# Attention stage of a decoder layer on one Trainium2 core: the last group's projection weights split once, the convolution's weights parked in free tiles

## The chip, the cores and the metric

The kernel runs on one core of a Trainium2 chip. The metric is the device time of one execution in microseconds (us); the median of three runs stands for a version. The engines are named as in the profile: PE does matmuls, PEld is its weight load, DVE, ACT and POOL work on tiles in on-chip memory, SP only issues DMAs. Each engine has its own queue and takes its instructions in the order that the program gives them; semaphores tell one engine that another is done.

## The reference, cut to what matters

One decoder layer works on 1024 positions of width 1024, all in float32. The part around the change is the mixing sub-layer:

```python
h = modulate(rms_norm(x, g_mix[l]), sh2, sc2)
b_g, c_g, u, q, k, v, z_conv, z_attn = jnp.split(h @ w_in[l], IN_OFFSETS, axis=-1)
y_conv = (b_g * short_conv(c_g * u, conv_w[l])) @ w_conv_proj[l]
q, k = apply_rope(q, cos, sin), apply_rope(k, cos, sin)
y_attn = sliding_window_attention(q, k, v, sinks[l]) @ w_attn_proj[l]
merged = jax.nn.sigmoid(z_conv) * y_conv + jax.nn.sigmoid(z_attn) * y_attn
x = x + gt2[:, None, :] * (merged @ w_out[l])
```

Attention has 16 heads of 64 in 4 groups of 4; a block of 128 positions sees itself and the block before it.

## The kernel before, in words

**Precision.** Every float32 matrix product is made of three matmuls on a high and a low part of each operand (`mm3`, L138, L140, L142). The parts are made by `split` (L106 and L107): ACT casts the high part, DVE subtracts it from the source for the low part. A weight block of 512 KB is loaded by `load_st` (L114) into one of four staging tiles `wr`, and `Weights` splits it into two tiles: four instructions, two on ACT and two on DVE. Loads through `parts_tile` put the parts into the 8 tiles `w`; with `tiles=` they go to tiles `t` of the pool "T", which has 28 and holds almost everything of this stage.

**The attention loop.** 32 units, (group g, block n), run through a software pipeline with a turn for each value of `s`, 0 to 36. In a turn PE does, in this order:

- stage c of unit s-3: the scores (L1031); DVE and ACT then make maximum and exponentials (L1042, L1048), POOL scales them (L1060)
- stage b of unit s-2: transposes q and k (L1010), which ACT and DVE split for the next turn's stage c
- stage a of unit s: q, k and v, 24 matmuls (L975 to L977); the last one is in turn 31
- some pieces of the output projection from the list `fill` (`proj_piece`): two a turn, one from turn 29 on, three from turn 33 on; a piece is 6 matmuls, and DVE adds it to `yat` (L1132)
- stage e of unit s-5: probabilities times v (L1097, L1098)
- stage d of unit s-4: transposes the probabilities (L1074), which ACT and DVE split for the next turn's stage e

The input of stage a, `h`, lies in 16 tiles of T, 8 for each half of the positions. The first half is last read in turn 27, the second in turn 31. When a group has finished a half, its 8 pieces enter `fill`; the pieces of group 3's first half are (3,0,0) to (3,0,7), those of the second half (3,1,0) to (3,1,7). The projection weights of a group are two blocks, `wap[g, 0]` and `wap[g, 1]`, and every half loads and splits both anew into two tiles of T each: `next_wap` runs when the piece before a block's first one has been issued, so 16 such loads in all.

**After the loop** comes `load_wc(0)`: four blocks of the convolution's projection weights through `wr`, split into the `w` tiles, which stage a's weights of group 3 hold until turn 31. Then `load_y(1)`, `conv_proj(0, 0)` and `conv_proj(1, 0)` (24 matmuls each), the eight pieces (3,1,*), and the other `conv_proj`. `load_y(0)`, 8 loads of 512 KB into T for the first half of the convolution's result, is called in turn 29 already. Each `conv_proj` also loads two stored gates (L1149) into the small tiles `r` and combines the branches on DVE (L1159 to L1161).

**What sets the order.** On PE the order is that of the code. On ACT, DVE, POOL and SP a scheduler sets it: it orders by its own estimate of when inputs and free tiles are there, so an instruction may stand ahead of its place in the code, and an engine waits whenever the estimate was too early. Each queue is served strictly in order: an ACT instruction that waits for a DMA holds every ACT instruction behind it.

Of the kernel before, what the change touches and what calls it, by code (L numbers as in the profile page):

```python
# [8 lines left out]
F32 = mybir.dt.float32  # L9
# [16 lines left out]
NKV = 4  # L26
# [9 lines left out]
def tile_macaron_layer(  # L36
# [19 lines left out]
    nc = tc.nc  # L56
# [12 lines left out]
    def nm(s):  # L69
        uid[0] += 1  # L70
        return f"{s}_{uid[0]}"

    def bank():
        return ps.tile([P, 512], F32, tag="ps", name=nm("ps"), bufs=8)
# [4 lines left out]
    def tile_t(dt=F32R, shape=(P, 2, HALF)):  # L79
        return act.tile(list(shape), dt, tag="T", name=nm("t"), bufs=28)  # L80

    def tile_c(dt, shape=(P, 1024)):
        return tile_t(dt, shape)
# [11 lines left out]
    def f32(t):  # L95
        return t.bitcast(F32)
# [4 lines left out]
    def pair_of(t):  # L101

        return t[:, 0, :], t[:, 1, :]
# [8 lines left out]
    def load_st(src):  # L112
        st = wgt.tile([P, 1024], F32, tag="wr", name=nm("wr"), bufs=4)
        nc.sync.dma_start(st[:, : src.shape[1]], src)  # L114
        return st
# [15 lines left out]
    def load_w(src, lo_engine=nc.vector, tiles=None):  # L131
        return Weights(load_st(src), src.shape[1], lo_engine, tiles)

    def mm3(outs, w, xs, start, stop):

        wh, wl = w
        for o, (xh, xl) in zip(outs, xs):
            mm(o, wh, xh, start=start, stop=False)  # L138
        for o, (xh, xl) in zip(outs, xs):
            mm(o, wh, xl, start=False, stop=False)  # L140
        for o, (xh, xl) in zip(outs, xs):
            mm(o, wl, xh, start=False, stop=stop)  # L142
# [437 lines left out]
    def load_last(hid):  # L580
        out = []
        for jj in range(2):
            out.append([])
            for h in range(2):
                t = tile_t()
                nc.sync.dma_start(f32(t), hid.last[jj][h])
                out[jj].append(pair_of(t))
        return out
# [43 lines left out]
    with tc.tile_pool(name="f1", bufs=2) as tmp:  # L632
# [150 lines left out]
        last = load_last(hid)  # L783
# [163 lines left out]
        for k in range(4):  # L947
            t = tile_t()
# [5 lines left out]
    with tc.tile_pool(name="att", bufs=2) as tmp:  # L954
# [5 lines left out]
        def load_group(g):  # L960
            lo_engine = nc.gpsimd if g == 0 else nc.vector
            wq[g] = [
                Weights(load_st(wqkv[g, kp]), 768, lo_engine,
                        )
                for kp in range(4)
            ]
# [36 lines left out]
        def stage_b(g, n):  # L1003

            u = st[g, n]
            if n == 0:
                kts[g] = tile_c(F32R), tile_c(F32R)
            o = bank()
            for i in range(3):
                nc.tensor.transpose(  # L1010
                    o[:, i * P : (i + 1) * P], u["r"][:, i * P : (i + 1) * P], ident
                )
            qt = sum_tile(HALF, F32R)
            qh, ql = qt[:, 0:256], qt[:, 256:512]
            split(qh, ql, o[:, 0:256])
            kh, kl = (t[:, n * P : (n + 1) * P] for t in kts[g])
            split(kh, kl, o[:, 256:384])
            u["q"] = (qh, ql)
# [46 lines left out]
        def stage_d(g, n):  # L1065

            u = st[g, n]
            nkb = 1 if n == 0 else 2
            ph, pl = tile_c(F32R), tile_c(F32R)
            for kb in range(nkb):  # L1070
                o = bank()
                for j in range(4):
                    at_col = (j % 2) * 2 + j // 2
                    nc.tensor.transpose(  # L1074
                        o[:, at_col * P : (at_col + 1) * P],
                        u["p"][:, j * 256 + kb * P : j * 256 + (kb + 1) * P], ident,
                    )
                split(ph[:, kb * 512 : (kb + 1) * 512], pl[:, kb * 512 : (kb + 1) * 512], o)
            u["pt"] = (ph, pl)
# [32 lines left out]
        wapt = {}  # L1112

        def next_wap(g, h, db):
            wapt["next"] = load_w(wap[g, db // 4], tiles=[tile_t(), tile_t()])

        def proj_piece(g, h, db):

            if db % 4 == 0:
                wapt[0] = wapt.pop("next")  # L1120
            o = bank()
            ah, al = at[g, h]
            for pr in range(2):
                c0 = pr * 512 + (db % 4) * P
                mm3([o], wapt[0](c0), [(ah[:, pr, :], al[:, pr, :])],
                    pr == 0, pr == 1)
            if db % 4 == 3 and fill:
                next_wap(*fill[0])
            if g == 0:
                nc.scalar.copy(yat[db][h], o)  # L1130
            else:
                nc.vector.tensor_tensor(yat[db][h], yat[db][h], o, op=ALU.add)  # L1132

        wc, yparts, stored = {}, {}, {}
# [3 lines left out]
        def load_y(h):  # L1138
            for i in range(KT):
                t = tile_t()  # L1140
                nc.sync.dma_start(f32(t), ycv[i][h])
                yparts[i, h] = pair_of(t)

        def load_wc(dq):
            wc[dq] = [load_w(wcp[g, dq]) for g in range(4)]
# [23 lines left out]
        n_units = len(units)  # L1169
        for s in range(n_units + 5):  # L1170
            def at_(k):
                return units[s - k] if 0 <= s - k < n_units else None
            if at_(3):
                stage_c(*at_(3))
            if at_(2):
                stage_b(*at_(2))
            if at_(0):
                g, n = at_(0)
                if n == 0:
                    load_group(g)  # L1180
                stage_a(g, n)
            if s == n_units - 3:
                load_y(0)

            for _ in range(2 if s < n_units - 3 else 1 if s <= n_units else 3):
                if fill:
                    proj_piece(*fill.pop(0))
            if at_(5):
                stage_e(*at_(5))
                g, n = at_(5)  # L1190
                if n % 4 == 3:
                    if not fill:
                        next_wap(g, n // 4, 0)
                    fill += [(g, n // 4, db) for db in range(8)]
            if at_(4):
                stage_d(*at_(4))
        load_wc(0)
        load_y(1)
        conv_proj(0, 0)
        conv_proj(1, 0)  # L1200
        while fill:
            proj_piece(*fill.pop(0))
# [65 lines left out]
    last = load_last(hid)  # L1268
# [146 lines left out]
```

## Time and profile before

| what | value |
|---|---|
| median of three runs | 2280.16 us (2279.49 to 2284.03) |
| the profiled execution's own time | 2279.57 us |
| its span, first to last instruction | 2277.8 us |
| busy: PE, DVE, ACT, POOL | 97%, 74%, 47%, 17% of the span |
| mean granted PE clock | 0.989 of full speed |
| turns 29 to 36 of the loop, from the trace | 1352.58 to 1422.85 us |
| the eight pieces (3,1,*) | 1433.75 to 1451.74 us |

Times in the trace are us from the start of the span. A row of the time line gives start, duration, engine, source line, operation, the tiles written and read, and in brackets the idle time before it with the work that ended the wait. Durations of matmuls that follow each other overlap; the distance between their starts is what each costs (0.23 us for 128x512 at full clock). A row of a table by stretches gives the stretch, its length, the busy time and number of instructions of PE, PEld, DVE, ACT and POOL, the granted PE clock, the share of the DMA engines and GB/s.

### The profile page before, as it was taken

How to read it: one execution, taken by the hardware profiler on the slowest of the kernel's cores; microseconds unless marked ns; L12 is line 12 of the kernel's file. 1: busy time of each engine (PE TensorE's matmuls, PEld its weight loads, DVE VectorE, ACT ScalarE, POOL GpSimd, SP SyncE). 2: the span in 40 equal slices, each digit the busy share in tenths (PEclk: the TensorE clock that was granted, in tenths of full speed). 3: DMA queues.
4: the chain of work that ended last, by engine and by line, in shares of the span. 5: the costliest groups of instructions: out<-in, count | busy, mean ns of one | idle time of the engine just before them, and what ended most of it. 6: DMA issues, size and time to landing. Idle time of an engine off the chain costs nothing.

```text
span 2277.8 us, 30045 instructions
## 1 busy us (share of the span) xinstructions
PE 2202.4 (97%) x10392; PEld 1844.5 (81%) x10392; DVE 1682.2 (74%) x2982; ACT 1062.8 (47%) x2095; POOL 382.5 (17%) x429
## 2 busy tenths in 40 slices
PE   5899999999998999999999998999999999999997
PEld 3688888888887888888999996788888888888886
DVE  8997778767867776777477878455786776676876
ACT  4554444444446534343476555124644444454443
POOL 3000000005452000000344343002100000002644
PEclk9999999999999999999999999999999999999998
DMA  8265456599832534544221233554233553389932
GB/s 322 76 222 177 147 185 213 179 405 302 278 106 103 189 117 124 157 157 131 92 64 57 63 107 103 175 178 150 70 121 120 185 185 120 121 323 346 345 113 74
DMA packets 146744, 381.63 MB, mean 168 GB/s; under 512 B 20384, under 2 KB 22560, under 8 KB 146592
## 3 DMA queue, kind: packets, MB, share of 16 engines
q1 hardware_dynamic: 141984, 371.33, 46.5%
q0 software_dynamic: 4608, 8.39, 2.1%
q8 instruction: 81, 1.33, 0.2%
q14 instruction: 71, 0.58, 0.1%
HBM read 270.61 MB, written 109.05 MB: 167 GB/s over the span
## 4 chain that ended last, share of the span: by engine, by line
PE 88%; DVE 8%; DMA 2%; issue 1%; ACT 1%; POOL 1%; SPq 0%; POOLq 0%; DVEq 0%; ACTq 0%
PE ps L195 61%; PE ps L142 6%; PE ps L138 6%; PE ps L140 6%; PE ps L977 2%; PE ps L976 2%; PE ps L975 2%; DVE w L107 1%; PE ps L1031 1%; PE ps L1074 1%; DVE t L225 1%; DMA wr<-in_w2d_dram 1%; DVE t L107 1%; PE ps L1010 1%; POOL s L319 1%
## 5 line engine op out<-in xcount | busy, mean ns | idle before, releaser
L195 PE MATMUL ps<-t,w 128*128 128x512 f32 x6468 | 1468.9, 389 | 3.8 <-DVE r L405 3.0
L195 PEld LDWEIGHTS ps<-t,w 128*128 128x128 f32 x6468 | 1213.3, 188 | 258.9 <-DVE r L405 5.2
L106 ACT CAST w<-wr 128x512 fp32r<-128x512 f32 (+1 forms) x420 | 254.9, 612 | 484.7 <-PE ps L195 364.5
L107 DVE TENSOR_TENSOR w<-wr,w 128x512 fp32r<-128x512 f32 (+1 forms) x404 | 303.8, 759 | 141.7 <-ACT w L106 140.4
L515 POOL TENSOR_TENSOR x<-x,g 128x512 f32<-128x512 f32 x96 | 145.5, 1530 | 1058.4 <-DMA t<-hs 471.0
L106 ACT CAST w<-ws 128x512 fp32r<-128x512 f32 x231 | 143.5, 621 | 249.1 <-PE ps L195 200.3
L140 PE MATMUL ps<-t,w 128*128 128x512 f32 (+1 forms) x528 | 205.7, 390 | 5.6 <-DVE t L290 5.6
L107 DVE TENSOR_TENSOR w<-ws,w 128x512 fp32r<-128x512 f32 x231 | 160.4, 698 | 40.1 <-ACT w L106 39.7
L138 PE MATMUL ps<-t,w 128*128 128x512 f32 (+1 forms) x400 | 156.9, 392 | 7.0 <-ACT t L279 7.0
L142 PE MATMUL ps<-t,w 128*128 128x512 f32 (+1 forms) x400 | 154.9, 387 | 2.0 <-DVE w L107 2.0
L140 PEld LDWEIGHTS ps<-t,w 128*128 128x128 f32 x528 | 100.9, 191 | 27.9 <-DVE t L290 8.3
L344 DVE TENSOR_TENSOR x<-x,x 128x512 fp32r<-128x512 f32 x161 | 102.6, 684 | 3.0 <-ACT x L343 2.7
L225 DVE CUSTOM_DVE_ANT_0 wr<-wr,crow_act,v 128x1024 f32<-128x1024 f32 x56 | 71.7, 1281 | 36.1 <-DMA wr<-in_wada_dram 36.1
L343 ACT CAST x<-x 128x512 fp32r<-128x512 f32 x161 | 88.7, 621 | 20.6 <-DVE x L431 8.4
L138 PEld LDWEIGHTS ps<-t,w 128*128 128x128 f32 x400 | 76.7, 192 | 24.1 <-ACT t L279 9.6
L319 POOL TENSOR_TENSOR s<-s,q 128x512 f32<-128x512 f32 (+1 forms) x48 | 56.8, 1186 | 208.6 <-ACT q L315 196.2
L142 PEld LDWEIGHTS ps<-t,w 128*128 128x128 f32 x400 | 76.9, 192 | 17.2 <-DVE w L107 2.4
L569 DVE SCALAR_TENSOR_TENSOR x<-ps,mods,x 128x512 f32<-128x512 f32 (+1 forms) x104 | 72.9, 706 | 23.6 <-PE ps L195 13.3
L975 PE MATMUL ps<-w,t 128*128 128x384 f32 x256 | 88.2, 345 | 1.2 <-DVE vt L1000 1.2
L107 POOL TENSOR_TENSOR w<-wr,w 128x512 fp32r<-128x512 f32 (+1 forms) x16 | 21.5, 1355 | 398.6 <-ACT w L106 398.6
L977 PE MATMUL ps<-w,t 128*128 128x384 f32 x256 | 85.8, 335 | 0.0
L976 PE MATMUL ps<-w,t 128*128 128x384 f32 x256 | 85.7, 335 | 0.0
(150 smaller groups left out, 2802.3 us busy)
## 6 DMA issues: line engine op xcount, KB each, us to landing
t<-hs SPq DMA_DIRECT2D x140, 512.0 KB, 9.9
hs<-x SPq DMA_DIRECT2D x277, 256.0 KB, 4.5
wr<-in_wada_dram SPq DMA_DIRECT2D x56, 512.0 KB, 3.8
wr<-in_w1gu_dram SPq DMA_DIRECT2D x44, 512.0 KB, 4.7
wr<-in_w2gu_dram SPq DMA_DIRECT2D x44, 512.0 KB, 3.6
wr<-in_wbcu_dram SPq DMA_DIRECT2D x24, 512.0 KB, 4.1
wr<-in_w1d_dram SPq DMA_DIRECT2D x22, 512.0 KB, 7.5
wr<-in_w2d_dram SPq DMA_DIRECT2D x22, 512.0 KB, 7.5
```

Source lines behind the costliest of these rows:

```text
L106: nc.scalar.copy(hi, src)
L107: lo_engine.tensor_tensor(lo, src, f32(hi), op=ALU.subtract)
L138: mm(o, wh, xh, start=start, stop=False)
L140: mm(o, wh, xl, start=False, stop=False)
L142: mm(o, wl, xh, start=False, stop=stop)
L195: mm(o, a, b, start=first, stop=last, skip_group_check=True)
L225: nc.vector.tensor_tensor_reduce(out=st, in0=st, in1=crow_act, scale=1.0, scalar=v[:, C_BADA + i : C_BADA + i + 1], op0=ALU.mult, op1=ALU. ...
L344: nc.vector.tensor_tensor(f32r(t), t, f32(hi), op=ALU.subtract)
L515: nc.gpsimd.tensor_tensor(dst, dst, r, op=ALU.add)
L975: mm(o[:, :384], xh, wh, start=k == 0, stop=False)
L976: mm(o[:, :384], xh, wl, start=False, stop=False)
L977: mm(o[:, :384], xl, wh, start=False, stop=k == KT - 1)
```

## The change

Three things change, all in the attention loop. Turn 29 (`s == n_units - 3`) loads and splits both weight blocks of group 3 into four tiles of T, kept as `wapt["last"]`; `next_wap` loads nothing for group 3, and its 16 pieces use the kept parts. The same turn loads the four raw blocks of the convolution's weights into four tiles of T (`wc_raw`), without `wr`; they are split into the `w` tiles after the loop, as before, but from those tiles. And `load_y(0)` moves from turn 29 to turn 32 (`s == n_units`). No matmul is added, removed or moved in PE's order.

```diff
         def next_wap(g, h, db):
-            wapt["next"] = load_w(wap[g, db // 4], tiles=[tile_t(), tile_t()])
+            if g < NKV - 1:
+                wapt["next"] = load_w(wap[g, db // 4], tiles=[tile_t(), tile_t()])
 
         def proj_piece(g, h, db):
 
-            if db % 4 == 0:
+            if g == NKV - 1:
+                wapt[0] = wapt["last"][db // 4]
+            elif db % 4 == 0:
                 wapt[0] = wapt.pop("next")
...
             if s == n_units - 3:
+
+                wapt["last"] = [
+                    load_w(wap[NKV - 1, dq], tiles=[tile_t(), tile_t()]) for dq in range(2)]
+                wc_raw = [tile_c(F32) for _ in range(4)]
+                for g, t in enumerate(wc_raw):
+                    nc.sync.dma_start(t, wcp[g, 0])
+            if s == n_units:
                 load_y(0)
...
-        load_wc(0)
+        wc[0] = [Weights(t) for t in wc_raw]
         load_y(1)
```

Lines below the diff's first hunk have other numbers in the changed kernel: the addition to `yat` is L1135 there, the loads of `ycv` L1144, the loads into `wc_raw` L1191.

On SP's queue before, behind the first of the two sets of eight loads of `ycv` (whose last is the first row), stand the convolution's first four weight blocks, then the 16th and last load of projection weights, then two blocks of the convolution's second weights:

```order
L1141 DMA t_12661<-ycv_5940 128x1024
L114 DMA wr_13345<-in_wcp_dram 128x1024
L114 DMA wr_13353<-in_wcp_dram 128x1024
L114 DMA wr_13361<-in_wcp_dram 128x1024
L114 DMA wr_13369<-in_wcp_dram 128x1024
L114 DMA wr_13498<-in_wap_dram 128x1024
L114 DMA wr_13749<-in_wcp_dram 128x1024
L114 DMA wr_13757<-in_wcp_dram 128x1024
L1141 DMA t_13377<-ycv_5927 128x1024
```

Now the four blocks go straight into tiles `t`, with three blocks of the second weights around them, ahead of the first set of loads of `ycv`; the rope loads are those of turns 30 and 31:

```order
L980 DMA rope_12777<-in_rope_dram 128x96
L114 DMA wr_13733<-in_wcp_dram 128x1024
L980 DMA rope_12898<-in_rope_dram 128x96
L1191 DMA t_12663<-in_wcp_dram 128x1024
L1191 DMA t_12664<-in_wcp_dram 128x1024
L1191 DMA t_12665<-in_wcp_dram 128x1024
L1191 DMA t_12666<-in_wcp_dram 128x1024
L114 DMA wr_13741<-in_wcp_dram 128x1024
L114 DMA wr_13749<-in_wcp_dram 128x1024
L1144 DMA t_12994<-ycv_5926 128x1024
```

The four loads now stand where the eight of `ycv` stood, and those come behind them and behind two staging loads that need a free `wr`.

On ACT in turns 33 and 34 before, casts of the convolution's weights (`w<-wr`) stand ahead of the casts of stage d's transposes (`t_13119`) and of the projection weights for piece (3,0,0) (`t_13176`, `t_13177`):

```order
L106 CAST w_13355<-wr_13353 128x512
L106 CAST w_13356<-wr_13353 128x512
L1104 COPY s_13112<-ps_13103 64x256 x2
L1108 CAST t_13101<-s_13112 128x2x128
L106 CAST w_13363<-wr_13361 128x512
L106 CAST w_13364<-wr_13361 128x512
L106 CAST t_13119<-ps_13121 128x512
L106 CAST t_13119<-ps_13128 128x512
L106 CAST t_13176<-wr_13178 128x512
L106 CAST t_13177<-wr_13178 128x512
```

At the same place now:

```order
L1055 ACTIVATE es_13075<-es_13075 128x4
L1104 COPY s_13136<-ps_13127 64x256 x2
L1108 CAST t_13125<-s_13136 128x2x128
L106 CAST t_13143<-ps_13145 128x512
L106 CAST t_13143<-ps_13152 128x512
L1048 ACTIVATE t_13173,den_13175<-t_13173,negm_13174 128x256 x4
```

No cast of a weight stands in turns 33 to 36 any more.

On DVE in turn 31 before, the rows behind the low part of k (`t_12203`) run on through the softmax's denominators (L1056, L1057) and rope (L985 to L991) to v's low part (L1000), stage e's sum (L1105) and the low parts of the probabilities (`t_12928`):

```order
L107 TENSOR_TENSOR t_12203<-ps_12856,t_12202 128x128
L1056 TENSOR_TENSOR den_12838<-den_12838,es_12839 128x4
L1057 RECIPROCAL den_12838<-den_12838 128x4
L985 TENSOR_TENSOR u_12892<-ps_12865,rope_12890 128x320
L988 TENSOR_TENSOR q_12893<-ps_12865,rope_12890 128x5x32
L991 TENSOR_TENSOR q_12893<-ps_12865,rope_12890 128x5x32
L1132 TENSOR_TENSOR x_9028<-x_9028,ps_12903 128x512
L1000 TENSOR_TENSOR vt_12779<-ps_12744,vt_12779 128x64
L1105 TENSOR_TENSOR s_12920<-s_12920,ps_12911 64x256
L107 TENSOR_TENSOR t_12928<-ps_12929,t_12927 128x512
```

Now, from the same low part of k on (three more subtractions of weights stand just above these rows):

```order
L107 TENSOR_TENSOR w_13352<-t_12664,w_13352 128x512
L107 TENSOR_TENSOR t_12203<-ps_12864,t_12202 128x128
L1135 TENSOR_TENSOR x_9028<-x_9028,ps_12911 128x512
L107 TENSOR_TENSOR w_13357<-t_12665,w_13357 128x512
L1056 TENSOR_TENSOR den_12846<-den_12846,es_12847 128x4
L107 TENSOR_TENSOR w_13358<-t_12665,w_13358 128x512
L107 TENSOR_TENSOR w_13363<-t_12666,w_13363 128x512
L107 TENSOR_TENSOR w_13364<-t_12666,w_13364 128x512
L1000 TENSOR_TENSOR vt_12787<-ps_12752,vt_12787 128x64
L1057 RECIPROCAL den_12846<-den_12846 128x4
L1105 TENSOR_TENSOR s_12928<-s_12928,ps_12919 64x256
L107 TENSOR_TENSOR t_12936<-ps_12937,t_12935 128x512
```

All eight subtractions of the convolution's first weights now stand in turn 31, the last four ahead of v's low part and of the low parts of the probabilities that stage e of turn 32 reads. The four subtractions of group 3's projection weights stand in turn 29, behind its L1042.

## The prediction

> **What bounds the kernel now.** I read the page first: its first lines, and of the 40 slices the one of PE.
>
> ```profile
> span 2277.8 us, 30045 instructions
> PE   5899999999998999999999998999999999999997
> ```
>
> PE is the bound nearly everywhere; the 25th slice (1367 to 1424 us), the end of the attention loop, is one of the few with an 8. So I read that stage: the table by stretches, cut at the starts of turns 29 to 32, at the first piece of turn 33, at the first matmul of conv_proj(0, 0), and at both ends of the pieces (3,1,\*).
>
> ```profile
> 1352.58:1360.87 8.29, 8.29 (x59) 7.73 (x59) 6.32 (x22) 4.68 (x16) 3.38 (x7) 1.00 1.01 405
> 1360.87:1369.64 8.77, 8.77 (x63) 8.21 (x63) 6.87 (x23) 5.45 (x18) 2.52 (x6) 1.00 0.16 66
> 1369.64:1378.33 8.69, 8.69 (x61) 8.13 (x61) 6.56 (x23) 5.16 (x18) 5.11 (x11) 1.00 0.01 2
> 1378.33:1387.31 8.98, 6.13 (x53) 5.17 (x53) 8.26 (x25) 7.33 (x23) 0.88 (x2) 1.00 0.19 58
> 1387.31:1422.85 35.54, 27.48 (x144) 22.07 (x142) 27.65 (x61) 19.02 (x50) 10.71 (x16) 0.86 0.41 141
> 1422.85:1433.75 10.90, 10.90 (x50) 9.01 (x49) 2.85 (x6) 1.14 (x3) 0.73 (x1) 1.00 1.04 403
> 1433.75:1451.74 17.99, 14.21 (x49) 10.86 (x48) 12.88 (x21) 2.29 (x4) 0.00 (x0) 0.81 0.61 198
> 1451.74:1480.00 28.26, 28.26 (x126) 23.42 (x125) 12.07 (x18) 2.66 (x5) 0.00 (x0) 1.00 0.29 82
> ```
>
> PE is full in turns 29 to 31 and in the two conv_proj at 1422.85. It is idle for 2.85 us in turn 32, 8.06 us up to conv_proj and 3.78 us in the last row but one, and in the last two of these three rows the granted clock is below 1 as well. The waits of PE over 1352 to 1480 us name the lines, and the time line of PE the places (with the rows from which I take lengths below):
>
> ```profile
> PE ps L138 <- ACT t L106: 7.6, 2, 5.5
> PE ps L142 <- DVE t L107: 4.1, 3, 2.2
> PE ps L1031 <- ACT t L106: 2.1, 1, 2.1
> PE ps L1031 <- DVE t L107: 0.8, 1, 0.8
> ```
>
> ```profile
> 1385.06 0.38 PE L1031 MATMUL ps<-t,ws 64*128 64x256 f32 x2 [2.07 <-ACT t L106]
> ...
> 1392.48 1.04 PE L1074 MATMUL ps<-ident,t 128*128 128x128 f32 x8
> 1393.45 0.98 PE L1031 MATMUL ps<-t,ws 64*128 64x256 f32 x12
> 1394.35 0.50 PE L138 MATMUL ps<-t,t 128*128 128x512 f32 x1
> ...
> 1401.54 0.79 PE L138 MATMUL ps<-t,t 128*128 128x512 f32 x1 [5.52 <-ACT t L106]
> ...
> 1404.99 0.79 PE L142 MATMUL ps<-t,t 128*128 128x512 f32 x1 [2.23 <-DVE t L107]
> 1405.58 0.63 PE L138 MATMUL ps<-t,t 128*128 128x512 f32 x1
> 1406.01 0.63 PE L140 MATMUL ps<-t,t 128*128 128x512 f32 x1
> ...
> 1410.10 1.04 PE L1074 MATMUL ps<-ident,t 128*128 128x128 f32 x8
> ...
> 1410.89 0.47 PE L138 MATMUL ps<-t,t 128*128 128x512 f32 x1
> ...
> 1417.70 0.48 PE L138 MATMUL ps<-t,t 128*128 128x512 f32 x1
> ...
> 1421.88 0.29 PE L1097 MATMUL ps<-t,vt 128*128 128x256 f32 x1
> ...
> 1441.42 0.50 PE L138 MATMUL ps<-t,t 128*128 128x512 f32 x1 [2.07 <-ACT t L106]
> ...
> 1443.86 0.79 PE L142 MATMUL ps<-t,t 128*128 128x512 f32 x1 [1.71 <-DVE t L107]
> ```
>
> The waits at 1401.54 and 1404.99 are those of piece (3,0,0) for its weights, high part from ACT and low part from DVE; those at 1441.42 and 1443.86 are piece (3,1,4)'s for the same reason. After each pair the matmuls start 0.43 us apart (1405.58, 1406.01), not 0.23, until PE has worked for some us. Why ACT was late shows its time line, and SP's:
>
> ```profile
> 1398.86 1.14 ACT L106 CAST w<-wr 128x512 fp32r<-128x512 f32 x2 [1.26 <-DMA wr<-in_wcp_dram]
> ...
> 1400.86 1.15 ACT L106 CAST t<-wr 128x512 fp32r<-128x512 f32 x2
> ```
>
> ```profile
> 1350.11 4.10 SPq L1141 DMA_DIRECT2D t<-ycv  x8
> 1383.35 17.81 SPq L114 DMA_DIRECT2D wr<-in_wcp_dram  x4
> ```
>
> The eight loads of the convolution's result took eight tiles of T at 1350, 73 us before their use at 1422.85. Group 3's projection weights found no tile, so they lay unsplit in `wr`; the convolution's weights then waited for a `wr`, one after another from 1383 on; and ACT, whose order has their casts ahead of the projection's, stood still for each. The DMA is the head of a chain that ends at PE.
>
> **The change part by part.** The sum is made against the profiled execution (2279.57 us, span 2277.8); the median shown is 0.6 us above it.
>
> *Turns 33 to 36.* Group 3's weights are split in turn 29, and in turns 33 to 36 ACT and DVE no longer have a weight in their rows. If PE waits for nothing from 1387.31 to 1422.85, it has to do four sets of three pieces (4.18 each, 1417.70 to 1421.88), four stages e (0.97 each, from there to 1422.85), stage d once ahead of scores (0.97, 1392.48 to 1393.45) and twice ahead of pieces (0.79 each, 1410.10 to 1410.89), and one stage c (0.90, 1393.45 to 1394.35): 16.72 + 3.88 + 0.97 + 1.58 + 0.90 = 24.05, of 35.54. That is 11.5 us saved, slow clock included. What is late next is DVE: 27.65 busy in that stretch, less the splits of (3,0,0), (3,0,4) and (3,1,0) and of the four convolution blocks, which go elsewhere. The rows for a weight's low part, grouped by form over 1340 to 1425 us, give each:
>
> ```profile
> L107 DVE TENSOR_TENSOR t<-wr,t 128x512 fp32r<-128x512 f32 x10 | 7.5, 793 | 0.0
> L107 DVE TENSOR_TENSOR w<-wr,w 128x512 fp32r<-128x512 f32 x8 | 5.6, 724 | 3.8 <-ACT w L106 3.8
> ```
>
> Six at 0.79 and eight at 0.72: 27.65 - 4.7 - 5.8 = 17.1 of 24.05, a share of 71%, less than in turns 29 to 31 where PE was full (6.32 of 8.29 is 76%, 6.87 of 8.77 is 78%). So I count no wait here.
>
> *Pieces (3,1,\*).* Their weights stay from turn 29 on. The same 48 matmuls of the same size took 10.90 in the two conv_proj, here 17.99: 7.1 us saved. Between them DVE also adds in order behind waits for gate loads, but two conv_proj and six pieces fill the eight `ps` tiles, and the adds need only keep within that; in the last row of the table, with the same gate loads, PE waited for none of it. The gate loads stand behind the second set of `ycv` loads as before. I count nothing, with 0 to 2 us as bounds (the longest wait of PE in that stretch, 2.07).
>
> *Turns 29 to 32, where the splits go.* Turn 29 gets four low parts, 4 x 0.79 = 3.2 us, on a DVE that is busy for 6.32 of 8.29: 1.2 too much, which turn 30 with 1.9 free takes up. Stage c of turn 30 needs k's low part, which stands behind them; by the durations it comes just in time. 0 to 1.2 us, I take 0. Turn 31 gets eight at 0.72, 5.8 us, on 2.1 free, so DVE enters turn 32 some 3.7 late, with 8.26 to do there. Stage e of turn 32 reads the probabilities' low parts, which stand behind those eight; so PE waits in turn 32, as it does before for another reason. If DVE never idles over both turns and all its work counts, they take 6.56 + 5.8 + 8.26 = 20.6 instead of 8.69 + 8.98 = 17.67: 2.95 us lost. If no wait is left, 2.85 are gained. Not all of DVE's work stands ahead of what PE waits for last (k's low part for stage c of turn 33); going down the rows I come to 1.3 us lost, near the upper end because DVE hardly idles. That is an estimate from those rows.
>
> *What is moved on SP.* The four raw loads go out at about 1350, where the `ycv` loads did, and are read from 1372 on; those needed 8 issues in 4.10 us, these need 4. Cover 20 us. `load_y(0)` now stands behind two staging loads (each waits for a split of turn 29, by about 1360) and needs the second half of `h` (PE past stage a of turn 31, before 1378.33) and two of the tiles whose splits are in turn 31. So it issues from 1378 to 1385, and is needed at some 1413: the cover is still over 25 us, against 17.81 for four loads one after the other at 1383. Two loads of 512 KB, four casts and four subtractions are gone: nothing, ACT and DVE have room after turn 32.
>
> *Sum.* 11.5 + 7.1 - 1.3 = 17.3 us: 2279.57 - 17.3 = 2262.3 for a profiled execution, and with the 0.6 above it 2263 for the median.
>
> **The clock.** Three stretches of the table bear on what the wait of turn 32 costs:
>
> ```profile
> 1384.00:1386.00 2.00, 0.38 (x2) 0.19 (x2) 2.00 (x7) 1.47 (x5) 0.00 (x0) 1.00 0.72 213
> 1398.00:1400.00 2.00, 0.00 (x0) 0.00 (x0) 0.49 (x1) 1.14 (x3) 0.41 (x1) 0.64 0.09 35
> 1441.40:1443.80 2.40, 0.73 (x2) 0.30 (x2) 2.40 (x5) 0.49 (x1) 0.00 (x0) 0.82 0.57 148
> ```
>
> Waits of 2.07 and 0.78 with two matmuls between left the clock at 1.00; 2.07 and 1.71 with 0.73 of work between did not (0.82). I expect in turn 32 two waits of about 2 us with one piece (1.4 us) between, nearer to the first case. If the clock falls, some 13 matmuls at 0.20 more each cost 2.7 us. The Trainium skill, "TensorE: Matmul & The Clock Gate", section "Part 1: The HAM clock gate (the "warmup" mystery)", says that PE falls to half clock after at least one idle window of about 3.4 us of a free-running count. By that rule no fall would come here, since neither wait is that long; the trace disagrees in the last row above, where no unbroken 3.4 us of idle lay before the fall. By the rule the sum stays 17.3, by the rows it can be 14.6.
>
> **The rivals.**
>
> - *The clock falls in turn 32* (12%): the 2.7 us above, 2265.7. For it speaks the row at 1441.40, against it the row at 1384.00.
> - *DVE is the bound in turns 29 to 33* (14%): each wait makes the next. Then 2.95 instead of 1.3, 1.2 in turn 29, 2 at the gates and the clock's 2.7: 7.6 more, 2270. For it speak the 8.26 of 8.98 in turn 32; against it the 2.1 and 1.9 free in turns 30 and 31.
> - *No wait is left in turn 32* (5%): 2.85 gained instead of 1.3 lost, 2259.
> - *Another link is just as late* (4%): stage d's casts, behind the same DMA waits on ACT, hold stage e, or the convolution's weights are late from `t` too; the waits move instead of going, and under 4.5 us is left, 2276 to 2280. Against it: in the new rows no ACT cast of turns 33 to 36 waits for a DMA.
> - *Slower: the late `load_y(0)`* (3%). It was 73 us early, and is now in a queue behind loads that wait for splits. If SP is held until after 1427, the tiles land after 1435, PE stands before conv_proj(0, 0) for over 22 us, and that decides: from there on it is slower than before by over 4.6. At 1440 the time is 2290. Only a wait of SP for something of turn 36 could do this, and I find none in the rows.
>
> That the change does not do what it says is excluded by the program: 14 loads of projection weights are left of 16.
>
> **How the numbers follow.** The forecast with its small bounds holds 62%, and 2263 is its value. No wait left gives 2259, rounded down for the run-to-run half us to 2258.5; the second rival gives 2270. From 2258.5 to 2270 over 8 in 10 are held; left out are the last two rivals and the tail of the second. About 0.2% (4.6 us) is what a measurement of this kernel can tell from no change. Faster by more: the forecast, the first three rivals, less a little, 92%; within: 5%; slower: 3%.
>
> **What would show it.** In the changed profile PE has no wait at L138 or L142 for L106 or L107 of a weight; turn 32 shows waits at L1097/L1098 or a piece's first matmul, 3 to 5 us in turns 32 and 33; from the first piece of turn 33 to conv_proj(0, 0) 24 to 25 us; the pieces (3,1,\*) 10.9 to 11.2; the clock at 1.00 from 1387 on. It is wrong if waits of over 3 us stand in turns 33 to 36, if stage c of turn 30 waits, or if conv_proj(0, 0) waits for a DMA.

## The result, and the profile after

The changed kernel takes 2264.07 us (median of four runs, 2263.03 to 2266.09), the kernel before, beside it on the same chip, 2281.85: a ratio of 0.992, with a 95% interval of 0.9908 to 0.9932. The profiled execution took 2263.03 us, with a span 16.5 us shorter than before. From the page of the profile, its first line and the 40 slices of PE:

```profile
span 2261.3 us, 30036 instructions
PE   5899999999998999999999999999999999999997
```

The 25th slice, an 8 before, is a 9. The table by stretches, cut at the same places of the program as before (turns 29 to 32, turns 33 to 36, two conv_proj, and the pieces (3,1,\*)):

```profile
1352.91:1361.20 8.29, 8.29 (x58) 7.73 (x57) 7.86 (x24) 6.87 (x20) 1.12 (x3) 1.00 0.80 305
1361.20:1369.97 8.77, 8.77 (x62) 8.21 (x62) 7.38 (x26) 5.38 (x18) 4.63 (x9) 1.00 0.18 65
1369.97:1378.73 8.76, 8.76 (x62) 8.20 (x61) 8.53 (x25) 8.18 (x23) 4.04 (x7) 1.00 0.47 165
1378.73:1388.53 9.80, 6.61 (x54) 5.27 (x53) 9.74 (x30) 8.06 (x25) 3.62 (x6) 1.00 0.75 288
1388.53:1412.73 24.20, 24.20 (x144) 20.88 (x142) 19.55 (x51) 11.89 (x36) 8.41 (x16) 1.00 0.64 227
1412.73:1423.63 10.90, 10.90 (x50) 9.01 (x49) 2.13 (x4) 1.15 (x3) 0.74 (x1) 1.00 0.44 147
1423.63:1434.51 10.88, 10.88 (x49) 9.01 (x48) 10.68 (x18) 1.25 (x2) 0.00 (x0) 1.00 0.47 155
```

Read the second number (the stretch's length) against PE's busy time beside it: they are equal in every row but that of turn 32. Turns 33 to 36 went from 35.54 to 24.20 us, the pieces (3,1,\*) from 17.99 to 10.88, turn 32 from 8.98 to 9.80, and the clock is 1.00 throughout. From turn 29 to the end of the pieces that is 81.60 us after 99.16, 17.6 less; the span gained 16.5, so 1.1 us went elsewhere, outside these turns and pieces, in parts where PE does the same work. In the profiles of this study turn 29 begins anywhere from 1351.3 to 1355.0 us, though nothing ahead of it was changed in any of them. So I compare kernels by this stage, and by their medians. Two executions far from the rest, one of wc_raw (2782 us, granted clock 0.752) and one of the kernel before (3607 us, 0.576), are left out of the medians and ratios of the table further down.

From 1340 to 1470 us PE still waits at three places:

```profile
1381.24 0.50 PE L138 MATMUL ps<-t,t 128*128 128x512 f32 x1 [1.05 <-DVE vt L1000]
1384.45 0.39 PE L1098 MATMUL ps<-t,vt 128*128 128x256 f32 x1 [1.20 <-DVE t L107]
1387.43 0.86 PE L1031 MATMUL ps<-t,ws 64*128 64x256 f32 x10 [0.94 <-DVE t L107]
```

All three are in turn 32 and at the start of 33, and all end with DVE. The time line of DVE shows why:

```profile
1379.17 1.88 DVE L107 TENSOR_TENSOR w<-t,w 128x512 fp32r<-128x512 f32 x3
1380.98 0.21 DVE L1000 TENSOR_TENSOR vt<-ps,vt 128x64 fp32r<-128x64 f32 x1
...
1383.71 0.68 DVE L107 TENSOR_TENSOR t<-ps,t 128x512 fp32r<-128x512 f32 x1
```

The last three subtractions of the convolution's weights end at 1381.05, 2.3 us into turn 32, and v's low part (L1000), for which PE waits, stands right behind them. The matmul that waits reads only tiles `t`: what it lacks is the `ps` tile that L1000 still has to read. SP's queue:

```profile
1351.42 1.75 SPq L1191 DMA_DIRECT2D t<-in_wcp_dram  x4
1358.55 1.61 SPq L114 DMA_DIRECT2D wr<-in_wcp_dram  x2
1373.54 5.11 SPq L1144 DMA_DIRECT2D t<-ycv  x8
```

The late `load_y(0)` issues from 1373.5 to 1378.7; `conv_proj(0, 0)` starts at 1412.73 and waits for nothing.

### The profile page after: what moved, and what is told of

Read it like the earlier page. It is cut to its first block, busy times and chain, and to the rows that moved or that the text cites. A ratio compares the mean times of both kernels' runs of the same rounds, so it can differ in the third digit from the quotient of the medians.

```text
span 2261.3 us, 30036 instructions
## 1 busy us (share of the span) xinstructions
PE 2196.2 (97%) x10392; PEld 1842.2 (81%) x10392; DVE 1680.0 (74%) x2978; ACT 1061.2 (47%) x2091; POOL 382.3 (17%) x429
## 4 chain that ended last, share of the span: by engine, by line
PE 89%; DVE 7%; issue 1%; DMA 1%; ACT 1%; POOL 1%; SPq 0%; POOLq 0%; DVEq 0%; ACTq 0%
PE ps L195 63%; PE ps L138 6%; PE ps L142 6%; PE ps L140 6%; PE ps L977 1%; PE ps L975 1%; PE ps L976 1%; DVE w L107 1%; PE ps L1031 1%; DVE t L225 1%; PE ps L1074 1%; DMA wr<-in_w2d_dram 1%; DVE t L107 1%; POOL s L319 1%; DVE x L569 1%
## 5 line engine op out<-in xcount | busy, mean ns | idle before, releaser
L142 PEld LDWEIGHTS ps<-t,w 128*128 128x128 f32 x400 | 76.7, 192 | 17.3 <-DVE w L107 2.4
```

## The experiments

All twelve kernels do the whole computation. The table gives, in us, the stretches of each profile as above; the ratios are against runs of the kernel before on the same chip (median 2281.4 to 2282.9 us beside the other kernels). Labels are shortened to their words.

| kernel | 29-32 | 33-36 | conv | (3,1,\*) | sum | median | ratio, 95% |
|---|---|---|---|---|---|---|---|
| before | 34.7 | 35.5 | 10.9 | 18.0 | 99.2 | 2281.85 | 1 |
| changed | 35.6 | 24.2 | 10.9 | 10.9 | 81.6 | 2264.07 | 0.9908-0.9932 |
| changed, again | 35.6 | 24.2 | 10.9 | 10.9 | 81.5 | 2264.57 | 0.9915-0.9942 |
| y_only | 32.9 | 32.5 | 10.9 | 18.5 | 94.8 | 2279.31 | 0.9974-0.9993 |
| y_after_loop | 35.7 | 35.1 | 13.0 | 20.5 | 104.2 | 2286.36 | 1.0014-1.0033 |
| wc_raw | 35.6 | 28.3 | 10.9 | 17.8 | 92.6 | 2275.62 | 0.9958-0.9984 |
| wap_once | 35.6 | 24.2 | 10.9 | 10.9 | 81.5 | 2262.91 | 0.9891-0.9927 |
| first_half | 35.6 | 24.1 | 10.9 | 17.6 | 88.3 | 2269.64 | 0.9939-0.9968 |
| y_last | 36.7 | 24.2 | 10.9 | 10.9 | 82.6 | 2267.04 | 0.9918-0.9955 |
| wc_lo_pool | 37.0 | 25.2 | 10.9 | 10.9 | 84.0 | 2267.58 | 0.9914-0.9946 |
| raw_late | 34.5 | 28.0 | 10.9 | 10.9 | 84.3 | 2267.82 | 0.9926-0.9959 |
| half_raw | 33.3 | 26.0 | 10.9 | 10.9 | 81.1 | 2263.40 | 0.9909-0.9933 |
| raw_t34 | 32.9 | 29.4 | 10.9 | 10.9 | 84.1 | 2266.73 | 0.9920-0.9945 |
| raw_t35 | 32.9 | 24.9 | 10.9 | 10.9 | 79.5 | 2262.99 | 0.9904-0.9932 |

### Was it the tiles? (y_only, y_after_loop)

```diff
 y_only, from before
-            if s == n_units - 3:
+            if s == n_units:
                 load_y(0)
```

> Before, with one edit: load_y(0) is called in turn 32 instead of turn 29, so the eight tiles of T that it took at 1350 us stay free until then; group 3's projection weights are still loaded and split per half, the convolution's weights still go through wr. Theory of the prediction (the eight ycv tiles kept the weights unsplit): with the tiles free the weights are split before turn 33, the waits of 5.52 and 2.23 us in piece (3,0,0) go and with them most of the 11.5 us of turns 33 to 36; 2268 to 2272 us against 2280 to 2282. Rival (the weights are split late because of the place of the split in the program, not for want of a tile): the row of turns 33 to 36 stays at 33 to 36 us and the pieces (3,1,*) at 17 to 18; 2279 to 2283 us, and a PE wait of over 4 us at L138 for ACT is still there.

Measured 2279.31 us, the rival's time, but not its wait of over 4 us: the pair at (3,0,0) is 0.98 and 2.40 us here, and turns 33 to 36 take 32.5 us. On ACT the casts of three more convolution blocks had come to stand behind those of (3,0,0); before, three of the four stood ahead, now none:

```profile
1396.88 1.15 ACT L106 CAST t<-wr 128x512 fp32r<-128x512 f32 x2
1397.92 1.15 ACT L106 CAST w<-wr 128x512 fp32r<-128x512 f32 x2
```

That speaks for the place in the queue, yet does not settle it, since the `ycv` loads went out from 1362 on, still ahead of the weights' split. So the next kernel asks for their tiles last:

```diff
 y_after_loop, from before
-            if s == n_units - 3:
-                load_y(0)
...
         load_wc(0)
+        load_y(0)
         load_y(1)
```

> Before, with one edit: load_y(0) is called after the loop, behind load_wc(0), so that the eight tiles for the convolution's result are asked for after those of the projection weights and cannot be what keeps these unsplit (with the call in turn 32 they still landed at 1362 to 1375 us and were asked for first). Theory of the prediction (the eight ycv tiles kept the weights unsplit): piece (3,0,0) no longer waits 5.52 and 2.23 us, turns 33 to 36 take 24 to 28 us instead of 35.5; about 2269 to 2273 us. Rival (the place of load_w in the program: the weights are asked for by the piece before, and their casts stand behind those of the convolution's weights): the waits of PE at L138 and L142 for a weight stay at 6 us or more in sum, turns 33 to 36 take 32 us or more, 2277 to 2283 us. If the late loads themselves are what decides, PE waits for a DMA of ycv before conv_proj(0,0), and it is slower than before.

PE at piece (3,0,0), in conv_proj(0, 0), and at (3,1,4):

```profile
1400.50 0.79 PE L138 MATMUL ps<-t,t 128*128 128x512 f32 x1 [4.12 <-ACT t L106]
1403.95 0.80 PE L142 MATMUL ps<-t,t 128*128 128x512 f32 x1 [2.24 <-DVE t L107]
...
1426.46 0.50 PE L138 MATMUL ps<-t,w 128*128 128x512 f32 x1 [0.32 <-DMA t<-ycv]
...
1446.56 0.79 PE L138 MATMUL ps<-t,t 128*128 128x512 f32 x1 [5.68 <-ACT t L106]
```

SP's row of those loads:

```profile
1415.45 13.91 SPq L1141 DMA_DIRECT2D t<-ycv  x16
```

No `ycv` tile was ahead of the weights, and they were as late as before: piece (3,0,0) starts 49.0 us after turn 29 in both kernels. (PE waits 4.12 us for it instead of 5.52 because it came there later itself, by a fall of its clock; see the last section.) The prediction's reading of the cause is refuted; the rival, the place of the split in the queue, holds. The loads themselves were now late as well: three waits of 0.3 us for a DMA of `ycv`, 13.0 instead of 10.9 in the conv_proj, 5.68 at (3,1,4). These two stretches are 4.6 us longer than before, which makes this kernel slower. Turns 29 to 32 are longer too, by 0.9 us, but with the same waits as before and a clock of 0.97 instead of 1.00.

### Which part of the change carries the gain? (wc_raw, wap_once, first_half)

```diff
 wc_raw, from before: the raw tiles and the late load_y(0), projection weights per half
             if s == n_units - 3:
-                load_y(0)
+                wc_raw = [tile_c(F32) for _ in range(4)]
+                for g, t in enumerate(wc_raw):
+                    nc.sync.dma_start(t, wcp[g, 0])
+            if s == n_units:
+                load_y(0)
...
-        load_wc(0)
+        wc[0] = [Weights(t) for t in wc_raw]
```

> The change without its first half: the convolution's weights come into four raw tiles at turn 29 and load_y(0) moves to turn 32, but group 3's projection weights are loaded and split per half as before. Theory (two separate blockages: the wr loads in front of piece (3,0,0), and gate adds in front of the split of (3,1,4)): turns 33 to 36 fall from 35.5 to 24 to 26 us, the pieces (3,1,*) stay at 17 to 18 us with two waits of about 2 us and a clock near 0.8; 2269 to 2272 us. Rival (the per-half weights are late by themselves): waits of over 2 us at L138 or L142 for a weight stay in turns 33 to 36 too; 2274 to 2281 us.

The rival came true. Turns 33 to 36 by stretches, PE and DVE at piece (3,0,0):

```profile
1389.79:1418.07 28.28, 25.29 (x143) 20.57 (x142) 23.54 (x56) 15.04 (x42) 9.46 (x16) 1.00 0.33 117
```

```profile
1398.83 0.50 PE L138 MATMUL ps<-t,t 128*128 128x512 f32 x1 [0.30 <-ACT t L106]
...
1401.96 0.50 PE L142 MATMUL ps<-t,t 128*128 128x512 f32 x1 [2.40 <-DVE t L107]
```

```profile
1400.03 0.68 DVE L107 TENSOR_TENSOR t<-ps,t 128x512 fp32r<-128x512 f32 x1
1400.63 0.67 DVE L1132 TENSOR_TENSOR x<-x,ps 128x512 f32<-128x512 f32 x1
1401.23 1.28 DVE L107 TENSOR_TENSOR t<-wr,t 128x512 fp32r<-128x512 f32 x2
```

With no cast that waits for a DMA on ACT any more, the wait for the high part is 0.30 instead of 5.52 and 7.3 us of the stretch are gone. But the low part still comes 2.40 us late, because it stands behind the softmax maxima and an addition of the same turn: 28.28 - 24.20 = 4.1 us are what the late split costs with no DMA ahead of it.

```diff
 wap_once, from the changed kernel: the convolution's weights through wr as before
-                wc_raw = [tile_c(F32) for _ in range(4)]
-                for g, t in enumerate(wc_raw):
-                    nc.sync.dma_start(t, wcp[g, 0])
...
-        wc[0] = [Weights(t) for t in wc_raw]
+        load_wc(0)
```

> The change without its raw tiles for the convolution: group 3's projection weights loaded and split once in turn 29, load_y(0) in turn 32, the convolution's weights through wr as before. Theory (what cost the time was ACT's and DVE's queue, with projection weights behind casts that wait for the wr loads): with the projection weights split early the wr tiles come free early too, the convolution's weights arrive well before their casts, and the time is the changed kernel's, 2262 to 2266 us; turns 33 to 36 about 24 us, pieces (3,1,*) 10.9. Rival (the one-after-another loads through wr stay slow wherever they stand, so the raw tiles carry part of the gain): ACT still waits for DMA in front of its convolution casts, stage e of turn 32 or 33 waits behind them, and 3 to 10 us of the 17 are lost: 2267 to 2274 us.

The theory's numbers, to 0.1 us of the stage. SP's queue here:

```profile
1359.02 21.62 SPq L114 DMA_DIRECT2D wr<-in_wcp_dram  x5
```

The `wr` tiles, no longer held by projection weights, take the convolution's blocks from 1359 on instead of 1383, and ACT waits once, for 0.9 us. The raw tiles add nothing once the projection weights are split early. So the 7.3 and the 4.1 us hold only where the raw tiles come first: here the early projection weights bring both without them. Both kernels have the late `load_y(0)`, which by itself brings 3.0 of the 11.3 us (y_only); no kernel splits the weights early without it.

```diff
 first_half, from the changed kernel
-            if g < NKV - 1:
+            if (g, h) != (NKV - 1, 0):
                 wapt["next"] = load_w(wap[g, db // 4], tiles=[tile_t(), tile_t()])
...
-            if g == NKV - 1:
+            if (g, h) == (NKV - 1, 0):
                 wapt[0] = wapt["last"][db // 4]
```

> The changed kernel, but only the first half's pieces (3,0,*) use the weights kept from turn 29; the second half loads and splits both blocks anew, as before. It separates the two large terms. Theory (11.5 us of turns 33 to 36 and 7.1 us of the pieces (3,1,*) are separate stalls): turns 33 to 36 take 24 to 25 us as in the changed kernel, the pieces (3,1,*) 17 to 18.5 us with two waits of about 2 us at piece (3,1,4) and a slow clock behind them; 7 us more than the changed kernel, 2269 to 2273 us. Rival (the second stall came from queues that were still late from the first): with turns 33 to 36 free of waits, the weights of (3,1,4) come in time, the pieces (3,1,*) take 11 to 13 us, 2264 to 2266 us.

```profile
1390.55:1414.69 24.14, 24.14 (x143) 20.88 (x142) 20.41 (x52) 12.91 (x38) 8.89 (x16) 1.00 0.53 194
...
1425.60:1443.24 17.64, 13.86 (x50) 10.62 (x48) 12.28 (x20) 2.28 (x4) 0.00 (x0) 0.81 0.46 149
```

The two large terms are separate stalls: the first is gone, the second is there in full, with the same waits of 2.07 and 1.71 us as before and the same clock of 0.81. What holds (3,1,4) is again the place of its split, as ACT shows:

```profile
1432.08 0.62 ACT L106 CAST x<-q 128x512 fp32r<-128x512 f32 x1 [2.38 <-DVE q L1164]
1432.61 1.13 ACT L106 CAST t<-wr 128x512 fp32r<-128x512 f32 x2
```

The weights' casts (`t<-wr`) stand behind those of two conv_proj (`x<-q`), which wait for DVE's L1164, and follow them at once. In the kernel before the order is the same. There DVE had also stood 7.12 us for a gate load; here it waited for no gate up to that cast, and the stall is as long, so it needs no late gate.

### Is the late load covered? (y_last)

```diff
 y_last, from the changed kernel
-            if s == n_units:
-                load_y(0)
...
+        load_y(0)
         load_y(1)
```

> The changed kernel with load_y(0) called after the loop instead of in turn 32: its eight loads then stand behind all that SP has to issue for turns 29 to 36. It measures the cover of the rival that was to make the change slower (late ycv loads). By the prediction's cover (SP is held by nothing of turn 36, and eight loads take 10 to 13 us from about 1387): the last lands before 1405 us, conv_proj(0,0) at about 1413 waits for nothing, and the time is the changed kernel's, 2262 to 2266 us. By the rival: SP or the tiles are held until turn 36 is done, the loads start after 1400, PE waits 3 to 12 us for a DMA before conv_proj(0,0), and the time is 2267 to 2276 us.

```profile
1386.34 22.10 SPq L1144 DMA_DIRECT2D t<-ycv  x16
```

SP issued the loads from 1386.3 on, and conv_proj(0, 0) waited for nothing. So the change could issue them 13 us later than it does without a wait in conv_proj(0, 0). The stage is 1.0 us longer, all of it in turn 32 (PE waits 1.50 us for k's low part instead of 0.94, and 0.42 for its high part). The median, 2267.04, is above what I expected; of the 3 us over the changed kernel the stage shows one, and the rest has no cause shown.

### What do the eight subtractions cost? (wc_lo_pool, raw_late, raw_t34, half_raw, raw_t35)

```diff
 wc_lo_pool, from the changed kernel
-        wc[0] = [Weights(t) for t in wc_raw]
+        wc[0] = [Weights(t, 1024, nc.gpsimd) for t in wc_raw]
```

> The changed kernel with one more edit: the eight subtractions that make the convolution weights' low parts in turn 31 (0.72 us each on DVE) are put on POOL. Theory (PE's remaining waits of 1.05, 1.20 and 0.94 us in turns 32 and 33 come from DVE entering turn 32 some 3.7 us late behind those eight): these waits go, 2 to 3.2 us less than the changed kernel, 2260.5 to 2262.5 us. Rival (turn 32 has its own DVE bound, 8.3 us of work in 9, or POOL is slower at this and its own work is late): the waits of PE in turns 32 and 33 stay at 2 to 4 us in sum, and the time within 1 us of the changed kernel's, 2263 to 2266 us.

Neither: slower than the changed kernel, by 2.4 us in the stage and 3.5 in the median (where the two intervals overlap). POOL, DVE, PE and a row of the table by stretches, in turns 31 to 33:

```profile
1374.33 5.05 POOL L107 TENSOR_TENSOR w<-t,w 128x512 fp32r<-128x512 f32 x4
...
1384.49 2.51 POOL L107 TENSOR_TENSOR w<-t,w 128x512 fp32r<-128x512 f32 x2
```

```profile
1385.47 1.61 DVE L1052 TENSOR_TENSOR es<-negm,v 128x4 f32<-128x4 f32 x1
1387.01 2.01 DVE L107 TENSOR_TENSOR t<-wr,t 128x512 fp32r<-128x512 f32 x2
```

```profile
1389.40 1.07 PE L1031 MATMUL ps<-t,ws 64*128 64x256 f32 x10 [2.65 <-DVE t L107]
```

```profile
1390.00:1393.00 3.00, 3.00 (x14) 2.39 (x11) 2.90 (x12) 1.52 (x6) 1.29 (x3) 0.50 0.62 175
```

POOL needs 1.26 us for one, and while it works some of DVE's own rows grow (last section), so that PE waits 2.65 us for k's low part where it waited 0.94; the clock then falls to 0.50.

```diff
 raw_late, raw_t34 and raw_t35, from the changed kernel; T is 0, 2 and 3
             if s == n_units - 3:
...
-                wc_raw = [tile_c(F32) for _ in range(4)]
-                for g, t in enumerate(wc_raw):
-                    nc.sync.dma_start(t, wcp[g, 0])
+            if s == n_units + T:
+                wc_raw = [tile_c(F32) for _ in range(4)]
+                for g, t in enumerate(wc_raw):
+                    nc.sync.dma_start(t, wcp[g, 0])
```

With T = 0 the four stand ahead of `load_y(0)`, otherwise that stays in turn 32, ahead of them.

> The changed kernel with the four raw loads of the convolution's weights called in turn 32 instead of 29. The eight subtractions on DVE then stand half in turn 32 behind its softmax and half in turn 33, instead of all in turn 31. Theory (the 3.2 us of PE waits in turns 32 and 33 are DVE's lateness from those eight): the waits of turn 32 (1.05 and 1.20) go, turn 33 has DVE time to spare, and 1 to 2.5 us less than the changed kernel is left in the stage from 1352 on: about 2262 us. Rival (the eight cost the same wherever they stand, since turn 32 has 8.3 us of DVE work in 9 of its own): the waits move into turns 33 and 34 and stay at about 3 us in sum; 2264 us, and if a wait of over 2 us is followed by a slow clock, 2266.

The rival, and worse: the waits are smaller than in the changed kernel up to stage c of turn 33 (0.97 and 0.38 us), but the first piece of turn 33 waits 0.98 and stage c of turn 34 1.37, and after the first of these the clock falls, 28.0 us in turns 33 to 36.

> The changed kernel with the four raw loads of the convolution's weights called in turn 34, behind load_y(0): the eight casts on ACT and eight subtractions on DVE then stand in turns 34 and 35, where PE has long rows of pieces and DVE is idle for a third of the time, and none stands in turns 31 to 33. Theory (the cost of the change in turns 29 to 32 is the eight subtractions standing where DVE is full, in turn 31 as in turns 32 and 33): PE waits in turns 32 and 33 fall from 3.2 to about 1 us, none comes back later, the stage from turn 29 to conv_proj(2,0) takes 79.5 to 80.5 us instead of 81.6; 2262 to 2263 us where the changed kernel takes 2264 to 2265. Rival (ACT's and DVE's queues move as a whole, so that what is taken out of turn 31 is waited for in turns 34 to 36 or before conv_proj(0,0)): the stage takes 81.5 us or more, 2264 us or more.

Turns 29 to 32 fell by 2.7 us as the theory has it, and turns 33 to 36 rose by 5.2: the rival in sum. PE and the clock:

```profile
1406.08 0.33 PE L1074 MATMUL ps<-ident,t 128*128 128x128 f32 x1 [0.64 <-POOL t L1060]
1407.88 2.23 PE L1074 MATMUL ps<-ident,t 128*128 128x128 f32 x7 [1.48 <-POOL t L1060]
```

```profile
1408.00:1411.00 3.00, 2.87 (x10) 2.22 (x11) 1.90 (x4) 1.44 (x3) 0.73 (x2) 0.53 0.96 380
```

Five subtractions stood ahead of the last reciprocal (L1057), which POOL's scaling and then stage d wait for. Waits of 2.5 us in all (0.42 at stage e among them); the other 2.7, by subtraction, I put down to the slow clock.

```diff
 half_raw, from the changed kernel
-                wc_raw = [tile_c(F32) for _ in range(4)]
+                wc_raw = [tile_c(F32) for _ in range(2)]
...
+            if s == n_units + 2:
+                wc_raw += [tile_c(F32) for _ in range(2)]
+                for g in (2, 3):
+                    nc.sync.dma_start(wc_raw[g], wcp[g, 0])
```

> The changed kernel with two of the four raw loads in turn 29 as in the change and two in turn 34: four subtractions in turn 31, four in turn 34 or 35. Theory (DVE has about 2 us free in turn 31, and what goes beyond that is waited for in turn 32): four at 0.72 are 2.9, so under 1 us of lateness is left, PE waits in turns 32 and 33 come to 1 to 1.8 us in sum, between the changed kernel's 3.2 and that with all loads in turn 34; about 2263 us. Rival (any subtraction in turn 31 stands ahead of the rows that stage e of turn 32 reads, so order counts, not the amount): 2.5 to 3.2 us of waits stay, 2264 us.

In between as the theory has it in turns 29 to 32 (33.3 us, one wait of 1.41 for ACT), but 1.8 us came back in turns 33 to 36. The stage is 0.4 shorter than the changed kernel's, the time the same.

> The changed kernel once more, on the same chip and in the same rounds as the two others, as the measure for them: 2262 to 2266 us, and the stage from turn 29 to conv_proj(2,0) 81.6 us as in its first profile. If the stage differs by over 0.3 us between the two profiles, differences of that size between the other kernels' stages mean nothing.

81.54 after 81.60: here the stage repeats to 0.1 us, while the medians of the two sets differ by 0.5.

> The changed kernel with the four raw loads of the convolution's weights called in turn 35. With the call in turn 34, turns 29 to 32 took 32.9 us instead of 35.6, but five subtractions stood ahead of the last softmax denominators (L1057), POOL's scaling and with it stage d of turn 35 waited 2.1 us, and the clock fell: 29.4 us in turns 33 to 36 instead of 24.2. Here all eight subtractions stand behind the last L1057, the first four ahead of the low parts that stage e of turn 36 reads. Theory (only what stands ahead of a row that PE is about to wait for costs anything): turns 29 to 32 take 32.9 us again, turns 33 to 36 24.2 to 25.5, the stage 79 to 80.5 us instead of 81.5; 2261 to 2263 us, a little faster than the changed kernel, though hardly more than a measurement can tell. Rival (the splits are now so late that stage e of turn 36 or conv_proj(0,0) waits for them, or the raw loads come too late behind those of ycv): turns 33 to 36 take 27 us or more, PE waits of over 1.5 us in sum at L138 for t or w, 2264 to 2268 us.

```profile
1351.61:1384.51 32.90, 31.93 (x232) 29.31 (x232) 28.38 (x91) 23.72 (x74) 11.95 (x23) 1.00 0.45 161
1384.51:1409.37 24.86, 24.42 (x144) 20.95 (x143) 23.00 (x57) 17.41 (x47) 7.95 (x15) 1.00 0.68 239
```

The theory: with all eight behind the last reciprocal (L1057), 2.7 us are won in turns 29 to 32 and 0.7 given back. The stage is 2.0 us shorter than the changed kernel's. In the median, 2262.99 us with a ratio of 0.9904 to 0.9932, that can't be told from the changed kernel's 2264.57 and 0.9915 to 0.9942.

## Why the prediction was right, point by point

*Turns 33 to 36.* 11.5 us predicted, 35.54 - 24.20 = 11.3 measured. The size was right, and it didn't hang on the cause, since it was worked out from what PE has to do when it waits for nothing. A step of the reasoning was wrong: "Group 3's projection weights found no tile, so they lay unsplit in `wr`". With the tiles free (y_after_loop) they lay unsplit just as long. What keeps them is their place: they are asked for by the piece before and stand in ACT's and DVE's queues behind rows of the same turn. The chain with a DMA at its head is real, but taking it away first brings 7.3 of the 11.3 (wc_raw); 4.1 stay with that place, and moving the split without the raw tiles brings all (wap_once). Had the change only taken the DMA away, the prediction's reasoning would have been 4 us too high.

*DVE as the next bound in turns 33 to 36.* I had 17.1 us of work for it; it was 19.55: DVE brings four rows left over from turn 32 with it, about 2 us. PE waited for none all the same.

*Pieces (3,1,\*).* 7.1 predicted, 7.1 measured, and a stall of its own, by the place of (3,1,4)'s split (first_half).

*Turns 29 to 32.* 1.3 us lost predicted, 0.9 measured. Where was right (stage e of turn 32 and the rows around it, 3.2 us of waits where 3 to 5 was said), the shape not: three waits of about 1 us instead of two of about 2. The subtractions took 0.68 each from the raw tiles, by the rows grouped by form, not 0.72:

```profile
L107 DVE TENSOR_TENSOR w<-t,w 128x512 fp32r<-128x512 f32 x8 | 5.3, 682 | 0.2 <-ACT w L106 0.2
```

Turn 29's four cost nothing, as taken. That the loss comes from those eight ahead of turn 32's rows is shown by raw_t35, where it turns into a gain of 1.8: near the rival with no wait left, though not in this change.

*SP.* No cost, as taken. `load_y(0)` issued five us earlier than I had it, and y_last shows 13 us more of cover. The slower rival is a real mechanism (y_after_loop is slower than before), but it came with loads that start at 1415; at 1386 (y_last) no wait for them was left.

*The clock* stayed at 1.00, so that rival did not come; with no wait over 1.20 us this run says little of what makes it fall. The row at 1384.00, which spoke against a fall, was weak evidence: in y_after_loop PE waited in the same way and the clock did fall (last section). The fall's price was well judged: in raw_t34 2.7 us are left for it when the waits are taken off.

*The sum:* 17.3 predicted, 17.6 in the stage, 16.5 in the span and 17.8 in the medians.

## What to carry to other kernels

When an engine waits for a small product of another engine, look at what stands ahead of that product in its queue before asking for more buffers: here tiles that were asked for last changed nothing for the split (y_after_loop), its place cost 4 us with no DMA ahead of it, and casts held by a DMA ahead of it 7 more. Work that is moved out of one full stretch must be put behind the last row that the bound engine waits for, not merely into a stretch with idle time: the same eight subtractions cost 5.2 us in turns 33 to 36 when five of them stood ahead of one reciprocal, and 0.7 when none did. Compare such versions by the stage in the trace, which came back to 0.1 us in the one repeat, and not by the time alone, which here can't tell 2 us; and look at the clock in each stretch first, since a fall moved turns 29 to 32 by 0.9 us between two kernels with the same waits.

## What the runs showed of the hardware

**The same wait may or may not be followed by a slow clock, and a fall needs no long wait.** The kernel before and y_after_loop give PE the same work in turns 31 and 32, and PE waited alike there: 2.07 us, two matmuls, then 0.78 or 0.79. Before, the clock stayed at 1.00; in y_after_loop it fell to 0.50. In raw_late PE worked for 1.74 us from 1384 to 1388 instead of 1.16, with no wait over 0.98 us, and the clock fell too. The tables by stretches of before, of y_after_loop and of raw_late:

```profile
1383.00:1387.00 4.00, 1.16 (x12) 0.84 (x12) 3.85 (x12) 2.42 (x9) 0.00 (x0) 1.00 0.42 131
```

```profile
1382.00:1386.00 4.00, 1.16 (x8) 0.96 (x10) 3.85 (x12) 2.42 (x9) 0.00 (x0) 0.87 0.37 131
1386.00:1388.00 2.00, 2.00 (x13) 1.68 (x10) 1.34 (x2) 1.45 (x3) 1.90 (x3) 0.50 0.01 4
```

```profile
1384.00:1388.00 4.00, 1.74 (x16) 1.17 (x16) 3.54 (x11) 3.93 (x12) 0.51 (x1) 1.00 1.03 412
1387.00:1390.00 3.00, 1.96 (x4) 1.15 (x5) 2.91 (x7) 2.98 (x7) 2.51 (x3) 0.67 0.62 244
```

So neither the longest wait nor the share of idle time alone decided it. The Trainium skill, "TensorE: Matmul & The Clock Gate", section "Part 1: The HAM clock gate (the "warmup" mystery)", counts in free-running windows of about 3.4 us: that the same idle time may or may not tell fits a window whose phase a kernel can't see, but that the window must be idle does not, if idle means without work, as in raw_late no wait of a whole us stood there. That it is the phase is not shown; what the pair of kernels shows is that the idle time alone doesn't settle it.

**POOL and DVE hold each other up.** DVE in the changed kernel, for the two rows shown of wc_lo_pool above; POOL's row in wc_lo_pool beside the second of them; and POOL in raw_t34, alone and beside DVE's subtractions:

```profile
1385.82 0.15 DVE L1052 TENSOR_TENSOR es<-negm,v 128x4 f32<-128x4 f32 x1
1385.89 1.29 DVE L107 TENSOR_TENSOR t<-wr,t 128x512 fp32r<-128x512 f32 x2
```

```profile
1387.15 0.72 POOL L1109 TENSOR_TENSOR t<-s,t 128x256 fp32r<-128x256 f32 x1
```

```profile
1393.77 1.84 POOL L1060 TENSOR_SCALAR t<-t,den 128x256 f32<-128x256 f32 x4 [2.35 <-PE ps L1031]
...
1405.30 3.44 POOL L1060 TENSOR_SCALAR t<-t,den 128x256 f32<-128x256 f32 x4 [8.98 <-DVE den L1057]
```

DVE's 128x4 row at L1052 took 1.61 us instead of 0.15 and ended with POOL's two subtractions (1387.08 and 1387.00); the two subtractions from `wr` behind it took 2.01 instead of 1.29, longer by the 0.72 of POOL's L1109 beside them. DVE's rows of 128x512 that read `ps` kept their 0.68 or 0.69. In raw_t34 it was the other way round: the four scalings of POOL took 3.44 us instead of 1.84, longer by 1.60, while DVE's three subtractions beside them kept their length (0.65, and 1.28 for two). The Trainium skill, "Trainium Architecture — The Big Picture", section "What this means for kernel authors", says that these two engines share a port pair and that it is an exclusive lock; the trace agrees, in that each time one side stood until the other's rows were done, which did not grow themselves, and rows from `ps` kept their length.
